# Dense attention scores in one place of two PSUM banks, banded attention with two banks of value sums: another split of the eight banks in a two-layer hybrid encoder on one core

## The chip, the cores and the metric

The kernel runs on one core of a Trainium2 chip. Time is device microseconds of one execution. The kernel before was run three times: 2706.91, 2704.07 and 2705.36 us, so its median is 2705.36 us. One further execution was recorded by the hardware profiler; it took 2709.95 us, and its span, from the first to the last instruction of the program, is 2707.9 us.

## The reference

`x` is 1024 tokens by 1024 features in float32. There are two layers. Each normalises `x`, projects it through one wide matrix, and cuts the result into four groups of four heads:

```
y_a = mla_mixer(...)    # A: latent attention, every query sees all 1024 keys
y_b = diff_mixer(...)   # B: per head two softmaxes over all 1024 keys, w = p0 - lam * p1
y_c = swa_mixer(...)    # C: keys within 128 of the query, with a sink logit
y_d = na_mixer(...)     # D: 8 x 16 neighbourhood on the 64-wide token grid, with a bias table
x = x + concat(norm(y_a), y_b, norm(y_c), norm(y_d)) @ w_out
x = x + square(relu(norm(x) @ w_up)) @ w_down
```

A last normalisation follows. A and B are called dense here, C and D banded. A softmax takes the row's largest score off before the exponential; the kernel finds it as the minimum of the negated scores.

## The kernel before

Each float32 operand of a product is kept as a high and a low part, so that a product is three matmuls per block of 128 rows (`passes`, lines 219 to 224). Half a projected tile is 8 blocks, or 24 matmuls of 512 columns.

In one layer `attention` goes through these stages. Two waves of three tiles make the queries, keys and values of B. Then B runs, then D, then C, then A; beside each of them runs a *fill*: products that the groups after it need. B has the latent projections of A (`proj_latent`) and the projections of D (`proj_d`) as its fill; D has the projections of C (`proj_c`, eight half tiles) and then the second step of A's latents (`latent_up`); C and A have the first half of the output projection (`groups_bd`). `weave` (line 545) puts the calls in turn, a few steps of the main work and then a few of the fill. Behind it a list scheduler sets the final order of each engine's instructions: it takes what is ready by priority (B and D have a lead over their fill), and gives a tile its place in a pool when the place is free. On the chip each engine then runs its list strictly in that order, and waits where an operand or a place is not ready.

PSUM has eight banks of 128 x 512 float32. `banks(mm=2, tr=2, sb=3, pv=1)` at line 426 divides them once for B, D, C and A together: two for products and small matmuls (`mm`), two for transposed probabilities (`tr`), three for scores (`sb`), one for sums of values (`pv`). A tile of one kind waits until an earlier tile at the same place has been read.

Dense attention is done by query tiles of 128 rows. `softmax` (lines 803 to 816) takes the 1024 keys as two halves, each with a bank of its own: matmuls (one per half in B, three in A), then on VectorE (DVE) a scaled copy to `p` that also keeps the running minimum (line 812). The second half starts from the first one's minimum. Then one exponential on ScalarE (ACT) runs over all 1024 (line 815). In B a query tile has two softmaxes; `cb` is the factor for the second one, ACT scales it (line 898) and GpSimd (POOL) adds the two. `dense` then transposes two query tiles together in four steps (`tr`), ACT and DVE make their high and low parts (`pth`, `ptl`), and TensorE (PE) multiplies them by the values (`pv`, lines 834 and 835).

Banded attention (`banded`, lines 966 to 1027) has eight query tiles with at most 384 keys each. Scores of four tiles are made ahead. For key block `kb`, `parts` transposes the probabilities of the up to three query tiles that see it, and `apply` adds their products to a bank of value sums that covers four query tiles. With one such bank the second half can only start when the first is read out: the parts of key blocks 3 and 4 are kept in `held` and applied a second time after that. `zeroed` (line 1032) starts a bank with a matmul of zeros. D's bias tile has six slots of 128 x 128, since a query tile at the edge needs two neighbouring slots of another kind.

Of the kernel before, what the change touches and what calls it, by code (L numbers as in the profile page):

```python
# [21 lines left out]
P = 128  # L22
S = 1024
# [55 lines left out]
def neighbours():  # L79
# [8 lines left out]
    out = np.full((P, 6, P), -1)  # L88
    for slot, ok in enumerate((row_ok & (ck >= c), row_ok, row_ok & (ck < c), row_ok, row_ok, row_ok)):
        at = (rk - r + 7) * 31 + 8 * (slot % 3 - 1) + ck - c + 15  # L90
        out[:, slot] = np.where(np.broadcast_to(ok, (P, P)), at, -1)
# [56 lines left out]
class Trunk:  # L148
# [232 lines left out]
    def attention(self, l):  # L381
# [42 lines left out]
        with ExitStack() as stack, ExitStack() as att:  # L424
            self.ap = att.enter_context(sbuf("att"))
            with self.banks(mm=2, tr=2, sb=3, pv=1):
                with sbuf("proj", "right") as self.pp:
# [10 lines left out]
                    def wave():  # L438
                        return [(self.bank(a), self.bank(b)) for a, b in (("sb", "sb"), ("sb", "tr"), ("tr", "pv"))]
# [24 lines left out]
                    fill = chain(proj_c(), self.latent_up(l, lat, rows, qa, ka, va))  # L464
                    self.weave(self.attn_d(l, qd, kd, vd, y["d"]), fill, self.RD, self.LD, every=self.EV[1])
                gout = lambda n: self.gout[n][:, l]
                self.tails.append(self.mix_group(mix, 2, y["d"], gout("na")))
                wa = stack.enter_context(sbuf("wa", "right"))
                wo = stack.enter_context(sbuf("wo", "right"))
                sums, w_out = [], d["w_out"][l]  # L470

                def groups_bd():

                    for m in range(self.EARLY):
                        x = wo.tile([P, S], F, tag="sum", bufs=self.EARLY, name="sum")
                        self.load(x, saved[m])
                        sums.append(x)
                    while None in mix[:4]:
                        yield True
                    for m, x in enumerate(sums):  # L480
                        ws = self.weights(w_out[m, 0])
                        for n in range(2):
                            ps = self.mm_ps()
                            self.product(ps, ws, mix[:4], n)
                            sl = slice(n * 512, n * 512 + 512)
                            self.tt(x[:, sl], ps, x[:, sl], ALU.add)
                            yield True
# [1011 lines left out]
```

## Time and profile before

| what | value |
|---|---|
| median of three runs | 2705.36 us |
| profiled execution | 2709.95 us, span 2707.9 us |
| PE busy | 2549.6 us, 94% of the span |
| DVE busy | 1943.0 us, 72% |
| ACT busy | 1439.8 us, 53% |
| POOL busy | 1130.9 us, 42% |
| B of the first layer, first to last score matmul | 83.1 to 329.4 us |
| D and C of the first layer, first to last score matmul | 330.0 to 480.0 us |
| A of the first layer, first to last score matmul | 480.1 to 614.5 us |
| the same three in the second layer | 1420.1 to 1668.4, 1669.1 to 1820.0, 1820.3 to 1953.0 us |

A matmul's own time in the profile holds its passage through the array: matmuls of 512 columns are shown with about 0.39 us each but start about 0.23 us apart. So PE can be shown busy while it idles a little between two of them, and the distance of starts is the better price.

### The profile page before, as it was taken

Reading aid. Unit: us, or ns where it says so; the run is one execution under the profiler, and the core shown is the slowest. Engines: PE = TensorE matmul, PEld = TensorE weight load, DVE = VectorE, ACT = ScalarE, POOL = GpSimd, SP = SyncE. Lnnn points to the kernel's source line nnn. Section 1 sums busy time; section 2 is a strip of 40 time slices with the busy share of each in tenths; the row PEclk is TensorE's granted clock in tenths of the full one; section 3 lists DMA queues with packets and bytes.
Section 4 is the critical chain, followed back from the end, with each engine's and each line's share of the span. In section 5 each row is a group of like instructions: output and inputs, shape, how many; then the busy total and the mean of one; then the engine's idle time right before and its main releaser. Section 6 shows DMA issues by size and latency. Waiting matters only on the chain.

```text
span 2707.9 us, 37502 instructions
## 1 busy us (share of the span) xinstructions
PE 2549.6 (94%) x12296; PEld 2112.5 (78%) x12296; DVE 1943.0 (72%) x3379; ACT 1439.8 (53%) x2601; POOL 1130.9 (42%) x754
## 2 busy tenths in 40 slices
PE   8989988999899998999999999889998999999997
PEld 6778876787778887888877788668876788878886
DVE  6777866774966668887567777677749666688775
ACT  4667756664534444444436776566635344444444
POOL 2555642201345554545434656321013455544442
PEclk9989988999999999999998899899999999999998
DMA  5534597222144457444244446962221444664431
GB/s 175 169 107 129 158 287 239 82 89 63 46 144 148 153 170 267 143 142 141 95 139 134 121 113 183 295 202 69 71 71 52 154 153 152 221 221 146 136 105 63
DMA packets 186931, 389.19 MB, mean 144 GB/s; under 512 B 23712, under 2 KB 26736, under 8 KB 186736
## 3 DMA queue, kind: packets, MB, share of 16 engines
q1 hardware_dynamic: 172912, 361.62, 43.2%
q10 hardware_dynamic: 13824, 25.17, 2.7%
q8 instruction: 97, 1.59, 0.2%
q14 instruction: 98, 0.80, 0.1%
HBM read 263.29 MB, written 123.41 MB: 143 GB/s over the span
## 4 chain that ended last, share of the span: by engine, by line
PE 73%; DVE 12%; DMA 6%; ACT 4%; issue 3%; POOL 1%; SPq 0%; DVEq 0%; ACTq 0%; POOLq 0%
PE u L222 8%; PE u L224 8%; PE u L223 8%; PE mm L222 5%; PE mm L223 5%; PE mm L224 5%; PE p L222 5%; PE p L223 5%; PE p L224 5%; PE sb L810 3%; PE tr L846 3%; DVE p L812 2%; DVE part L190 2%; PE pv L835 2%; PE pv L834 2%
## 5 line engine op out<-in xcount | busy, mean ns | idle before, releaser
L190 POOL TENSOR_TENSOR wl<-raw,wh 128x512 fp32r<-128x512 f32 x448 | 632.8, 1413 | 704.8 <-ACT wh L196 691.0
L196 ACT ACTIVATE wh<-raw 128x512 fp32r<-128x512 f32 x448 | 281.5, 629 | 576.2 <-PE u L223 310.9
L190 POOL TENSOR_TENSOR wl<-ws,wh 128x512 fp32r<-128x512 f32 (+1 forms) x112 | 147.3, 1316 | 461.0 <-ACT wh L196 436.1
L222 PE MATMUL u<-far,wh 128*128 128x512 f32 x768 | 301.8, 393 | 11.4 <-ACT ev L1242 8.3
L224 PE MATMUL u<-far,wl 128*128 128x512 f32 x768 | 300.6, 391 | 2.2 <-POOL wl L190 2.2
L190 DVE TENSOR_TENSOR raw<-raw 128x512 f32<-128x512 f32 x256 | 223.1, 877 | 109.1 <-POOL wl L190 55.6
L223 PE MATMUL u<-far,wh 128*128 128x512 f32 x768 | 300.6, 391 | 0.0
L190 DVE TENSOR_TENSOR ptl<-tr,pth 128x512 fp32r<-128x512 f32 (+2 forms) x384 | 238.3, 629 | 68.5 <-ACT pth L196 66.8
L815 ACT ACTIVATE p<-p,nm 128x1024 f32<-128x1024 f32 x192 | 220.2, 1147 | 92.3 <-DVE nm L812 91.6
L196 ACT ACTIVATE pth<-tr 128x512 fp32r<-128x512 f32 (+2 forms) x384 | 205.2, 546 | 108.5 <-PE tr L846 64.9
L222 PE MATMUL p<-far,wh 128*128 128x512 f32 x640 | 252.9, 395 | 7.5 <-DVE ev L190 7.5
L224 PE MATMUL p<-far,wl 128*128 128x512 f32 x640 | 251.5, 393 | 1.5 <-POOL wl L190 1.5
L223 PE MATMUL p<-far,wh 128*128 128x512 f32 x640 | 252.2, 394 | 0.0
L810 PE MATMUL sb<-stack 96*128 96x512 f32 x640 | 217.5, 422 | 22.1 <-DVE nm L812 21.4
L190 DVE TENSOR_TENSOR far<-act,far 128x512 fp32r<-128x512 f32 x224 | 207.3, 955 | 14.7 <-ACT far L196 14.7
L190 POOL TENSOR_TENSOR p<-p 128x1024 f32<-128x1024 f32 x64 | 154.0, 2411 | 129.6 <-ACT p L898 121.3
L222 PEld LDWEIGHTS u<-far,wh 128*128 128x128 f32 x768 | 145.3, 189 | 43.5 <-ACT ev L1242 9.1
L222 PE MATMUL mm<-xh,wh 128*128 128x512 f32 x416 | 170.9, 411 | 0.8 <-DVE part L190 0.3
L224 PEld LDWEIGHTS u<-far,wl 128*128 128x128 f32 x768 | 145.2, 189 | 33.5 <-POOL wl L190 3.0
L812 DVE CUSTOM_DVE_ANT_0 p<-sb,zero,nm 128x512 f32<-128x512 f32 x192 | 142.4, 743 | 37.7 <-PE sb L810 34.6
L223 PEld LDWEIGHTS u<-far,wh 128*128 128x128 f32 x768 | 145.4, 189 | 30.0
L223 PE MATMUL mm<-xl,wh 128*128 128x512 f32 x416 | 167.7, 403 | 0.0
(245 smaller groups left out, 6110.1 us busy)
## 6 DMA issues: line engine op xcount, KB each, us to landing
act<-acts SPq DMA_DIRECT2D x224, 256.0 KB
raw<-in_w_up SPq DMA_DIRECT2D x128, 256.0 KB
acts<-ev SPq DMA_DIRECT2D x128, 256.0 KB
raw<-in_w_down SPq DMA_DIRECT2D x128, 256.0 KB
acts<-ev ACTq DMA_DIRECT2D x96, 256.0 KB
ws<-in_w_in SPq DMA_DIRECT2D x76, 256.0 KB
rz<-drows SPq DMA_DIRECT2D x40, 256.0 KB
stack<-kd SPq DMA_DIRECT2D x32, 256.0 KB
```

Of the source, the lines that this page charges most:

```text
L190: (eng or self.nc.vector).tensor_tensor(out=out, in0=a, in1=b, op=op)
L196: nc.scalar.activation(hi, src, AF.Copy)
L222: mm(ps, w[0], x[0][:, sl], start=start, stop=False)
L223: mm(ps, w[0], x[1][:, sl], start=False, stop=False)
L224: mm(ps, w[1], x[0][:, sl], start=False, stop=stop)
L810: self.nc.tensor.matmul(ps, q[:, qt * P:(qt + 1) * P], k[:, sl], start=i == 0, stop=i == len(passes) - 1)
L812: self.nc.vector.tensor_tensor_reduce(out=p[:, sl], in0=ps, in1=self.zero[:, 0:1].bitcast(F).broadcast_to([P, 512]), scale=-scale, scalar= ...
L815: self.nc.scalar.activation(p, p, AF.Exp, bias=nm[:, 1:2], scale=-1.0, accum_out=z)
L834: nc.tensor.matmul(out, v[:, kt], h[:, sl], start=kt == 0, stop=False)
L835: nc.tensor.matmul(out, v[:, kt], lo[:, sl], start=False, stop=kt == 7)
L846: nc.tensor.transpose(t[:, k * 256 + i * P:k * 256 + (i + 1) * P], p[:, (j * 2 + k) * P:(j * 2 + k + 1) * P], self.ident)
```

## The change

- `softmax` takes one tile of 128 x 1024 that covers two neighbouring banks, writes both halves of the scores into it, and runs one VectorE instruction over 1024 elements with one minimum. `sb` has one such place in the dense stages.
- The banks are divided anew for each stage: `DENSE` (mm 2, tr 3, sb one place of two banks, pv 1) for the waves and B, `BANDED` (mm 2, tr 2, sb 2, pv 2) for D and C, and `DENSE` again for A. Three pools follow each other where there was one.
- `banded` opens the second half's bank at key block 3, while the first is still open, and applies every part once to each half that it belongs to. Nothing is held.
- The bias tile has five slots. An edge tile takes two of them that stand two apart, so `in1` of its VectorE instruction has a step, and the other operands are written as blocks of 128.

```
-            with self.banks(mm=2, tr=2, sb=3, pv=1):
-                with sbuf("proj", "right") as self.pp:
+            with sbuf("proj", "right") as self.pp:
+                with self.banks(**self.DENSE):
...
                     def wave():
-                        return [(self.bank(a), self.bank(b)) for a, b in (("sb", "sb"), ("sb", "tr"), ("tr", "pv"))]
+                        sb = self.bank("sb", (P, S))
+                        return [(sb[:, 0:512], sb[:, 512:S])] + [
+                            (self.bank(a), self.bank(b)) for a, b in (("tr", "tr"), ("tr", "pv"))]
...
-                    fill = chain(proj_c(), self.latent_up(l, lat, rows, qa, ka, va))
-                    self.weave(self.attn_d(l, qd, kd, vd, y["d"]), fill, self.RD, self.LD, every=self.EV[1])
...
+                banded = ExitStack()
+                banded.enter_context(self.banks(**self.BANDED))
+                fill = chain(proj_c(), self.latent_up(l, lat, rows, qa, ka, va))
+                self.weave(self.attn_d(l, qd, kd, vd, y["d"]), fill, self.RD, self.LD, every=self.EV[1])
...
+            self.weave(self.attn_c(l, qc, kc, vc, y["c"]), fill, self.RC, end=False, every=self.EV[2])
+            self.tails.append(self.mix_group(mix, 4, y["c"], gout("swa")))
+            banded.close()
+            with self.banks(**self.DENSE):
                 self.weave(self.attn_a(l, qa, ka, krd, va, y["a"]), fill, self.RA, self.LA, every=self.EV[3])
...
+    DENSE = dict(mm=2, tr=3, sb=1, pv=1)
+    BANDED = dict(mm=2, tr=2, sb=2, pv=2)
...
-        nm, p = self.col("nm", 2), self.ptile()
+        nm, p = self.col("nm"), self.ptile()
+        ps = self.bank("sb", (P, S))
         for n in range(2):
-            ps = self.bank("sb")
             sl = slice(n * 512, n * 512 + 512)
             for i, (q, k) in enumerate(passes):
-                self.nc.tensor.matmul(ps, q[:, qt * P:(qt + 1) * P], k[:, sl],
+                self.nc.tensor.matmul(ps[:, sl], q[:, qt * P:(qt + 1) * P], k[:, sl],
                                       start=i == 0, stop=i == len(passes) - 1)
-            self.nc.vector.tensor_tensor_reduce(
-                out=p[:, sl], in0=ps, in1=self.zero[:, 0:1].bitcast(F).broadcast_to([P, 512]), scale=-scale,
-                scalar=nm[:, 0:1] if n else 3e38, op0=ALU.add, op1=ALU.min, accum_out=nm[:, n:n + 1])
-        self.nc.scalar.activation(p, p, AF.Exp, bias=nm[:, 1:2], scale=-1.0, accum_out=z)
+        self.nc.vector.tensor_tensor_reduce(
+            out=p, in0=ps, in1=self.zero[:, 0:1].bitcast(F).broadcast_to([P, S]), scale=-scale,
+            scalar=3e38, op0=ALU.add, op1=ALU.min, accum_out=nm)
+        self.nc.scalar.activation(p, p, AF.Exp, bias=nm, scale=-1.0, accum_out=z)
...
-        pv = self.zeroed()
-        held = []
+        pv = {}
...
-            if kb in (3, 4):
-                held.append(part)
-            if kb <= 4:
-                apply(pv, 0, kb, part)
-            else:
-                apply(pv, 1, kb, part)
-            if kb == 4:
-                self.pv_out(pv, y, j, 0, grid)
-                pv = self.zeroed()
-                for i, p in enumerate(held):
-                    apply(pv, 1, 3 + i, p)
+            for half in range(2):
+                if half * 3 <= kb <= half * 3 + 4:
+                    if kb == half * 3:
+                        pv[half] = self.zeroed()
+                    apply(pv[half], half, kb, part)
+                    if kb == half * 3 + 4:
+                        self.pv_out(pv[half], y, j, half, grid)
...
-                bias = self.ap.tile([P, 6, P], F, tag="bias", bufs=1, name="bias")
+                bias = self.ap.tile([P, 5, P], F, tag="bias", bufs=1, name="bias")
...
-                    b0 = {0: 4, 7: 3}.get(i, 0)
-                    w = ps.shape[1]
+                    near = bias[:, {0: slice(2, 5, 2), 7: slice(0, 3, 2)}.get(i, slice(1, 4))]
+                    blocks = lambda t: t.rearrange("p (a b) -> p a b", b=P)
...
-                        out=p, in0=ps, in1=bias[:, b0:b0 + w // P].rearrange("p a b -> p (a b)"),
+                        out=blocks(p), in0=blocks(ps), in1=near,
```

The built programs give each place in PSUM. In `DENSE` of the first layer `sb` is banks 0 and 1, `tr` banks 2, 3 and 4, `pv` bank 5 and `mm` banks 6 and 7. In `BANDED` `sb` is banks 0 and 1, `mm` banks 2 and 3, `tr` banks 4 and 5, `pv` banks 6 and 7. So D's first products stand where B's last transposes stood. PE has 12088 matmuls before and after, DVE 384 instructions of line 812 before and 192 after.

The scheduler's order moves with it. The first place is PE where B ends and D begins, in the first layer. Lines 222 to 224 are products (`mm<-xh`, here of `proj_c`), 810 a half of B's scores, 846 transposes, 834 and 835 B's value sums, 982 D's scores. Before:

```order
L834 MATMUL pv<-pth,v 128x256
L835 MATMUL pv<-ptl,v 128x256
L846 MATMUL tr<-ident,p 128x128 x4
L810 MATMUL sb<-stack 128x512
L223 MATMUL mm<-xl_165,wh 128x512
L982 MATMUL sb<-stack 128x256 x2
L224 MATMUL mm<-xh_164,wl 128x512
L222 MATMUL mm<-xh_168,wh 128x512
L223 MATMUL mm<-xl_169,wh 128x512
L224 MATMUL mm<-xh_168,wl 128x512
L982 MATMUL sb<-stack 128x384 x2
```

Of the eight half tiles of `proj_c`, five stand ahead of D's first score and the sixth has begun, among B's last nineteen halves of scores. The same place of the changed kernel (scores at line 992, transposes 856, value sums 844 and 845, products 223 to 225, zeros 1036):

```order
L844 MATMUL pv<-pth,v 128x256
L845 MATMUL pv<-ptl,v 128x256
L844 MATMUL pv<-pth,v 128x256
L845 MATMUL pv<-ptl,v 128x256
L992 MATMUL sb<-stack 128x256 x2
L992 MATMUL sb<-stack 128x384 x2
L1036 MATMUL pv<-zero 128x512
L223 MATMUL mm<-xh_164,wh 128x512
```

This is the first product of `proj_c`: all eight half tiles stand behind B's last value sum. Between the last product of `proj_d` and this row there are 241 matmuls and no product: the scores of B's last 19 tiles (38 of line 820), 93 transposes, 96 value sums, and 14 others (D's first four scores, the zeros and nine small ones). The second layer's order is alike.

The second place is PE inside that stretch, where score tiles (line 820, two matmuls each in B) follow each other:

```order
L844 MATMUL pv<-pth,v 128x256
L845 MATMUL pv<-ptl,v 128x256
L856 MATMUL tr<-ident,p 128x128 x3
L820 MATMUL sb<-stack 128x512 x6
L856 MATMUL tr<-ident,p 128x128 x9
L820 MATMUL sb<-stack 128x512 x2
L844 MATMUL pv<-pth,v 128x256
```

Three tiles, x6, now stand right behind each other and all use banks 0 and 1; before, halves went round three banks.

52 lines of the change are left out of this document (25 added, 27 removed).

## The prediction

> **What bounds the kernel now.** I read the page's busy times first, then a table of the first layer by stage, then in each stage who waits for whom.
>
> ```profile
> span 2707.9 us, 37502 instructions
> ...
> PE 2549.6 (94%) x12296; PEld 2112.5 (78%) x12296; DVE 1943.0 (72%) x3379; ACT 1439.8 (53%) x2601; POOL 1130.9 (42%) x754
> ```
>
> ```profile
> core 0: us, PE busy (x) PEld busy (x) DVE busy (x) ACT busy (x) POOL busy (x), PEclk, DMA share, GB/s
> 150.00:175.00 25.00, 17.39 (x74) 13.62 (x73) 19.61 (x44) 16.45 (x27) 18.99 (x11) 0.73 0.40 105
> 175.00:288.00 113.00, 112.03 (x628) 95.73 (x626) 83.95 (x223) 83.77 (x138) 58.05 (x32) 1.00 0.40 119
> 288.00:330.00 42.00, 42.00 (x223) 35.62 (x224) 32.30 (x80) 28.43 (x45) 29.59 (x19) 1.00 0.52 144
> 330.00:362.00 32.00, 29.75 (x164) 26.01 (x163) 17.82 (x48) 19.07 (x46) 13.74 (x10) 0.95 0.94 254
> 362.00:438.00 76.00, 63.72 (x347) 52.05 (x346) 57.23 (x151) 52.93 (x138) 29.65 (x20) 0.93 0.96 298
> 492.00:631.00 139.00, 131.63 (x826) 112.96 (x825) 104.77 (x231) 90.63 (x160) 12.33 (x8) 1.00 0.23 68
> 675.00:700.00 25.00, 25.00 (x112) 20.64 (x111) 21.55 (x31) 13.52 (x23) 3.88 (x3) 1.00 0.19 65
> ```
>
> While B has products beside it (175 to 330) PE is busy in 154.0 of 155 us and DVE in three quarters: PE sets the pace. Where B lacked products (150 to 175) PE did 74 matmuls in 25 us, at a granted clock of 0.73. D with its latents (362 to 438) leaves PE 12.3 us open. The last row, 112 matmuls of 512 columns in 25 us, prices one at 0.223 us. The feed-forward half is not edited, so only the attention stages, about 83 to 631 us and 1420 to 1969 us, can move.
>
> B's pace, and how much of the products lay under B's end:
>
> ```profile
> 83.00:330.00 247.00, 54.17 (x128) 24.47 (x128) 0.95 0.44 129
> 288.00:330.00 42.00, 7.70 (x19) 3.53 (x19) 1.00 0.52 144
> ```
>
> ```profile
> 288.00:330.00 42.00, 26.10 (x81) 15.03 (x81) 0.00 (x0) 0.00 (x0) 1.00 0.52 144
> ```
>
> The first fence counts halves of B's scores (line 810): 128 in 247 us. A query tile has four, so 32 query tiles took 7.7 us each. The second counts matmuls that read `xh`, two of a product's three: 81 mean 121 matmuls, 27 us of products, in B's last 42 us.
>
> **The change part by part.** Rows for the prices, from the groups by line:
>
> ```profile
> L812 DVE CUSTOM_DVE_ANT_0 p<-sb,zero,nm 128x512 f32<-128x512 f32 x192 | 142.4, 743 | 37.7 <-PE sb L810 34.6
> L812 DVE CUSTOM_DVE_ANT_0 p<-sb,zero 128x512 f32<-128x512 f32 x192 | 129.1, 685 | 35.2 <-PE sb L810 9.7 <-POOL p L190 9.0 <-PE tr L846 8.0
> L812 DVE DVE_READ_ACCUMULATOR2_ANT nm<- 128x1 f32 x384 | 31.3, 82 | 0.0
> L815 ACT ACTIVATE p<-p,nm 128x1024 f32<-128x1024 f32 x192 | 220.2, 1147 | 92.3 <-DVE nm L812 91.6
> L815 ACT ACTIVATION_READ_ACCUMULATOR p<-p,nm 128x1 f32 x192 | 35.9, 187 | 0.0
> L898 ACT ACTIVATE p<-p,cb 128x1024 f32<-128x1024 f32 x64 | 72.9, 1143 | 12.1 <-DVE cb L897 11.1 <-DVE cb L896 0.7
> L196 ACT ACTIVATE pth<-tr 128x512 fp32r<-128x512 f32 (+2 forms) x384 | 205.2, 546 | 108.5 <-PE tr L846 64.9 <-PE tr L991 25.6 <-PE pv L1003 13.1
> L190 POOL TENSOR_TENSOR p<-p 128x1024 f32<-128x1024 f32 x64 | 154.0, 2411 | 129.6 <-ACT p L898 121.3 <-PE mm L222 4.1 <-PE sb L810 3.6
> ```
>
> *One minimum.* A softmax's DVE work is now 685 + 743 + 2 x 82 = 1592 ns. No row shows 1024 elements. Below, one such instruction cannot be shorter than 743 ns; above, it is two of 685 ns. The 384-column banded form (0.548 us median) against 0.685 us for 512 gives 1.07 ns a column, so I take 685 + 512 x 1.07 = 1.23 us, 1.31 with its read. That saves 0.28 us, 53 us of DVE over 192 softmaxes. In B, DVE is not the bound, so this buys nothing there; PE's products cover it.
>
> ```profile
> L1058 DVE CUSTOM_DVE_ANT_0 p<-sb,bias x64: 406/548/558, 333.4 to 1751.0; 128x384 f32<-128x384 f32 x48, 128x256 f32<-128x256 f32 x16
> ```
>
> *One place.* With three banks PE already idles for score places:
>
> ```profile
> PEld sb L810 <- DVE nm L812: 32.4, 36, 5.0
> ...
> PE sb L810 <- DVE nm L812: 21.4, 22, 4.6
> ```
>
> With one place the next tile waits for the whole minimum, about 1.5 us from the last score's start of passage to the release. In the changed order I summed PE's own work between one tile and the next, at the prices here: in a layer's B 26 to 29 of 64 tiles have less than 1.45 us there, some none. Behind a waiting score stand, on PE, transposes and value sums, and for those ACT and DVE. Outside the stretch treated next the shortfalls add up to 12 us; 7 of them lie around the present hole at 150 to 175 us, where PE waits anyway. I take +6 us a layer, bounds 0 and 12.
>
> The Trainium skill (Perfetto Trace Analysis, Optimizing Tensor Performance) says that independent groups of matmuls should go round different banks, so that one's read-out overlaps the next one's matmuls. The trace agrees as far as it goes, since the two waits above exist even with three banks; by the rule alone every one of 192 tiles could pay a whole 1.31 us, an estimate of 250 us where no other work stands between.
>
> *B's end without products.* `proj_c` now starts behind B's last transposes, since D's `mm` banks were B's `tr` banks. So 19 score tiles, 9.5 query tiles, run with no product beside them. What sets their pace then? ACT needs 2 x (1.147 + 0.187) + 1.143 + 2 x 0.546 = 4.9 us a query tile, DVE 2 x 1.31 plus two `ptl` of some 0.63, 3.9 us. The present kernel shows a short burst without products (between the `proj_d` and `proj_c` parts):
>
> ```profile
> 279.76 0.39 PE L810 MATMUL sb<-stack 96*128 96x512 f32 x1
> ...
> 282.84 0.94 PE L810 MATMUL sb<-stack 96*128 96x512 f32 x3
> ...
> 285.42 0.28 PE L834 MATMUL pv<-pth,v 128*128 128x256 f32 x1
> 285.54 0.28 PE L835 MATMUL pv<-ptl,v 128*128 128x256 f32 x1
> 285.66 0.60 PE L846 MATMUL tr<-ident,p 128*128 128x128 f32 x4
> ...
> 286.22 0.40 PE L810 MATMUL sb<-stack 96*128 96x512 f32 x1
> ```
>
> Seven halves start within 6.5 us, under 4 us a query tile, but that is what buffers allow for a moment. I take ACT's 4.9: 9.5 x 4.9 = 47 us, plus the last tile's way out (POOL 2.4, then four steps of transposes and parts at about 1.1), 7 us: 54. Lower bound 9.5 x 4.5 (ACT's reads hidden) + 5 = 48; upper bound today's pace, 9.5 x 7.7 + 7 = 80. Today's end takes 42 us, so +12 (+6 to +38). But it holds 9.5 tiles, not 19: what stands ahead is shorter by 4.75 query tiles. One costs PE 4 x 0.223 for scores, and per step four transposes at (0.60 - 0.27) / 3 = 0.11 and four value sums at 0.12, for two steps: 2.7 us. That is -13.
>
> *Products moved into D.* The 27 us of products now stand among D's heads, whose span today is 330 to 438, with 14.5 us of PE open by the table. Hidden entirely they cost 0, not at all 27. `latent_up` comes after them, and its loads need the places of `proj_c`'s operands, so nothing of it comes earlier; on SP its loads fall behind those of D's later heads, where the DMA share is 0.94 to 0.96. I take 27 - 13 = +14.
>
> *Two value banks, two score banks, five slots.* The bank of zeros is waited for like this:
>
> ```profile
> L1032 PE MATMUL pv<-zero x32: 376/483/774, 363.1 to 1844.5; 128*128 128x512 f32 x32
> ...
>   DVE y L190: 13.5, 17
>   DVE yc L190: 3.4, 9
> ```
>
> At most 17 us in the kernel, 8 a layer; a stall removed there lets the next transposes arrive, for which ACT and DVE are then late, so I take -4. The third score bank's loss is 0 to 3, taken as 2. The bias load is shorter by a sixth, and waits for it end in 7.4 us at most over both layers: nothing. The stepped operand on DVE could cost or save a few tens of ns in 16 edge tiles: nothing.
>
> *A.* 32 tiles a layer; 7 to 12 have too little work between, by 5 us (0 to 11). DVE gets 32 x 0.28 = 9 us lighter, and `tr` has a third bank, against waits for DVE and ACT in a stage where PE is shown idle 7.4 us of 139: -4 (-9 to 0). Sum of this and the part before: -1, from -17 to +14.
>
> **Sum.** A layer: +6 + 12 - 13 + 14 - 1 = +18 us; both: +36. The profiled execution, 2709.95, would become 2746; it lies 4.6 over the median of the runs, 2705.4, which would become 2741.
>
> **The rivals.**
>
> *B's end at today's pace.* If latency through `p`'s six places (score, minimum, exponential, factor, POOL's sum of 2.4 us, transposes) sets B and not ACT, the end takes 80 us: 26 more a layer, 2793. For it: the hole at 150 to 175 was as slow. Against it: there POOL was busy 19 of 25 us with other work, and the burst at 280 was fast.
>
> *D takes the products for nothing* (the other side). D's heads wait on DMA, DVE and each other and not on PE, so its open time swallows all 27 us, and then the value banks give their full 8 a layer, without a loss from the scores' third bank; of the score waits only 2 us remain, those around the present hole being swallowed too. The sum is 2 + 12 - 13 + 0 - 8 + 1 = -6 a layer, 2693. It decides from the point where less than about 3 us of the 27 stay visible. For it: the DMA share near 1, and D's pace of 27 us a head (108 by 4). Against it: the table shows 14.5 us of PE open, half of what it needs.
>
> *DVE was the bound.* Then its 53 us come out of the span: 2652. For it: the exponential waits 91.6 us for the minimum in the row of line 815. Against it: 154 of 155 us of PE.
>
> The Trainium skill (Perfetto Trace Analysis, Optimizing Scalar/DVE Operations) says that larger operations raise throughput where the engine is saturated, and that where it is not, but causes bubbles elsewhere, breaking instructions up may let work finish sooner. DVE's 72% puts this kernel on the second side, which speaks against the change.
>
> *The pieces cancel*: B's end takes 48 and the products cost 2, so 6 + 6 - 13 + 2 - 1 = 0: 2705. Nothing speaks for it but the size of the bounds.
>
> **How the numbers follow.** Forecast 0.49; B's end at today's pace 0.15; D takes all 0.16; DVE bound 0.06; cancelling 0.14. About 0.2%, 5.4 us, is what a measurement here can tell from no change. So slower 0.64, same 0.14, faster 0.22. All lower bounds together give 0 + 6 - 13 + 0 - 17 = -24 a layer, 2657; all upper bounds 12 + 38 - 13 + 27 + 14 = +78, 2861. The range of 8 in 10 is 2690 to 2795: it leaves out DVE as the bound, nearly half of the case with D, and what lies beyond a slow end. The forecast's own range is 2718 to 2765, half of each bound taken.
>
> **What would show it.** Right, if products (`mm<-xh`) are absent for some 50 us before D's first score, the score halves there keep 4.5 to 6 us a query tile, and waits of `sb` for `nm` grow from 54 to over 90 us. Line 812's successor should show about 1.23 us for 1024 elements. D's span should grow by 10 to 20 us with PE fuller; the waits of `pv<-zero` should vanish. It is wrong if PE stays full to B's last score, if the stretch takes under 45 us, or if A shortens by more than 8 us.

## The result, and the profile after

The changed kernel takes 2848.02 us (median of four runs, 2842.53 to 2853.89). The kernel before, run beside it, takes 2706.14 us. The ratio is 1.0521, with a 95% interval from 1.0495 to 1.0548: the change makes the kernel 5.2% slower. The forecast was 2741, the range 2690 to 2795. The direction was right, and the loss is four times as large: +142 us instead of +36. No rival that was written down gives it either.

The page of the changed kernel, its first two rows on the span and the engines:

```profile
span 2846.0 us, 37064 instructions
...
PE 2603.1 (91%) x12296; PEld 2141.2 (75%) x12296; DVE 1925.3 (68%) x2995; ACT 1440.1 (51%) x2601; POOL 1132.3 (40%) x754
```

The groups by line (busy us, mean ns of one, then idle time before them and what ended it):

```profile
L822 DVE CUSTOM_DVE_ANT_0 p<-sb,zero 128x1024 f32<-128x1024 f32 x192 | 234.2, 1220 | 129.5 <-PE sb L820 128.2 <-issue 0.3
L825 ACT ACTIVATE p<-p,nm 128x1024 f32<-128x1024 f32 x192 | 220.2, 1147 | 117.0 <-DVE nm L822 116.6
L820 PE MATMUL sb<-stack 96*128 96x512 f32 x640 | 208.7, 437 | 49.4 <-DVE nm L822 48.7
...
L820 PEld LDWEIGHTS sb<-stack 96*128 96x128 f32 x640 | 115.9, 202 | 84.8 <-DVE nm L822 69.5
```

The minimum over 1024 elements takes 1220 ns, as the estimate of 1.23 had it, and VectorE's scores cost 234.2 us where two halves cost 142.4 + 129.1. No gain from that saving is to be seen: the minimum now waits 128.2 us for scores, and scores wait 48.7 + 69.5 = 118 us for minima, where it was 54 (the rows of PE and of its weight loads added as in the prediction; in time they overlap, so such sums compare kernels and are not a loss in us).

The stages of the first layer, as one table of windows:

```profile
core 0: us, PE busy (x) PEld busy (x) DVE busy (x) ACT busy (x) POOL busy (x), PEclk, DMA share, GB/s
...
150.00:250.00 100.00, 87.28 (x428) 70.26 (x427) 65.23 (x135) 68.62 (x111) 52.26 (x29) 0.88 0.37 106
250.00:295.00 45.00, 45.00 (x238) 38.44 (x237) 26.11 (x50) 26.52 (x45) 23.25 (x13) 1.00 0.30 101
295.00:365.00 70.00, 47.83 (x241) 36.84 (x240) 45.35 (x92) 49.30 (x79) 27.17 (x12) 0.80 0.40 106
365.00:424.00 59.00, 58.16 (x293) 49.01 (x292) 29.84 (x71) 25.98 (x64) 25.91 (x20) 1.00 0.63 176
424.00:496.00 72.00, 53.58 (x283) 44.37 (x282) 48.23 (x123) 42.93 (x112) 23.65 (x17) 0.88 0.93 281
496.00:522.00 26.00, 21.60 (x123) 15.98 (x121) 20.41 (x64) 21.28 (x59) 7.71 (x6) 1.00 0.94 285
522.00:557.00 35.00, 26.14 (x121) 20.68 (x121) 20.42 (x38) 15.68 (x33) 10.48 (x5) 0.80 0.29 81
557.00:690.00 133.00, 124.36 (x745) 108.86 (x746) 90.23 (x148) 78.74 (x140) 12.34 (x8) 0.95 0.25 71
```

There are two holes. The first is B's end: 241 matmuls in 70 us (295 to 365), with none of `proj_c` among them, as the same window for the tile `xh` shows (its one matmul is the last before the stretch):

```profile
295.20:365.60 70.40, 0.24 (x1) 0.19 (x1) 0.00 (x0) 0.00 (x0) 0.81 0.40 105
```

B's last 38 halves of scores lie in the 55 us from 295 to 350 (the window for line 820); the other 15 us are the way out, in which hardly anything but transposes and value sums of the last tiles is left:

```profile
295.00:350.00 55.00, 16.29 (x38) 6.88 (x37) 0.81 0.35 98
```

The second hole is 522 to 557: 121 matmuls in 35 us, between C's last score (522.2) and A's first (557.2). Before, A's first score came at 480.1, right behind C's last at 480.0. The hole holds the transposes and value sums of C's last tiles, 24 matmuls of the output projection and a few small ones. For the operands of that projection (`mixh`, `mixl`) TensorE also waits in it:

```profile
541.73 1.11 PE L223 MATMUL mm<-mixh,wh 128*128 128x512 f32 x2 [3.19 <-ACT mixh L200]
543.84 0.79 PE L224 MATMUL mm<-mixl,wh 128*128 128x512 f32 x1 [1.00 <-DVE mixl L201]
...
546.61 0.79 PE L224 MATMUL mm<-mixl,wh 128*128 128x512 f32 x1 [1.55 <-DVE mixl L201]
```

The layer can be cut at four starts that every kernel has. From B's first score to D's first it takes 281.6 us against 246.9 (+35), from there to C's last score 157.6 against 150.0 (+8), from there to A's first score 35.0 against 0.2 (+35), and from there to the first matmul of the feed-forward 212.1 against 219.0 (-7). That is +70 in the first layer. In the second it is 687 us against 619, +68, with nearly the same four parts (+32, +10, +34, -8).

### The profile page after: what moved, and what is told of

It is laid out like the page before. It is cut to its first block, busy times and chain, and to the rows that moved or that the text cites. A ratio compares the mean times of both kernels' runs of the same rounds, so it can differ in the third digit from the quotient of the medians.

```text
span 2846.0 us, 37064 instructions
## 1 busy us (share of the span) xinstructions
PE 2603.1 (91%) x12296; PEld 2141.2 (75%) x12296; DVE 1925.3 (68%) x2995; ACT 1440.1 (51%) x2601; POOL 1132.3 (40%) x754
## 5 line engine op out<-in xcount | busy, mean ns | idle before, releaser
L822 DVE CUSTOM_DVE_ANT_0 p<-sb,zero 128x1024 f32<-128x1024 f32 x192 | 234.2, 1220 | 129.5 <-PE sb L820 128.2
L820 PE MATMUL sb<-stack 96*128 96x512 f32 x640 | 208.7, 437 | 49.4 <-DVE nm L822 48.7
L856 PE MATMUL tr<-ident,p 128*128 128x128 f32 x1024 | 169.7, 294 | 33.0 <-POOL p L191 17.4
L820 PEld LDWEIGHTS sb<-stack 96*128 96x128 f32 x640 | 115.9, 202 | 84.8 <-DVE nm L822 69.5
L223 PEld LDWEIGHTS u<-far,wh 128*128 128x128 f32 x768 | 145.2, 189 | 42.4 <-ACT ev L1246 9.1
L856 PEld LDWEIGHTS tr<-ident,p 128*128 128x128 f32 x1024 | 132.3, 152 | 54.2 <-POOL p L191 22.2
```

The source lines that it names most:

```text
L223: mm(ps, w[0], x[0][:, sl], start=start, stop=False)
L820: self.nc.tensor.matmul(ps[:, sl], q[:, qt * P:(qt + 1) * P], k[:, sl], start=i == 0, stop=i == len(passes) - 1)
L822: self.nc.vector.tensor_tensor_reduce(out=p, in0=ps, in1=self.zero[:, 0:1].bitcast(F).broadcast_to([P, S]), scale=-scale, scalar=3e38, op0 ...
L856: nc.tensor.transpose(t[:, k * 256 + i * P:k * 256 + (i + 1) * P], p[:, (j * 2 + k) * P:(j * 2 + k + 1) * P], self.ident)
```

## The experiments

Two causes are in question. **Seams**: three PSUM pools follow each other instead of one, so that nothing of a later pool would start before the earlier one's last work. **Places**: dense scores have one place of two banks instead of three banks that go round. The rivals to them are parts that were changed along: the length of the minimum, the value banks, the bias slots. In the table, B is its first to last score, D and C the first score of D to the last of C, A its first to last score, all of the first layer in us; "layer" runs from B's first score to the first matmul of the feed-forward, in both layers. Ratios are to the kernel before, run beside it.

| kernel | ratio, 95% interval | B | D, C | A | layer |
|---|---|---|---|---|---|
| before | 1 | 246 | 150 | 134 | 616 / 619 |
| changed | 1.0521, 1.0495 to 1.0548 | 267 | 158 | 133 | 686 / 687 |
| e1, both seams alone | 1.0307, 1.0286 to 1.0328 | 232 | 172 | 126 | 654 / 658 |
| f2, seam before D alone | 1.0218, 1.0189 to 1.0247 | 230 | 179 | 134 | 645 / 648 |
| e5, seam before A alone | 1.0124, 1.0092 to 1.0156 | 245 | 149 | 125 | 627 / 632 |
| e2, one place and one minimum, one pool | 1.0311, 1.0286 to 1.0335 | 291 | 215 | 134 | 661 / 658 |
| e6, one place and two minima, one pool | 1.0777, 1.0736 to 1.0818 | 341 | 204 | 157 | 721 / 720 |
| f1, two places and one minimum, one pool | 1.0396, 1.0371 to 1.0422 | 225 | 200 | 149 | 668 / 672 |
| f3, changed, but two single banks and two minima | 1.0330, 1.0314 to 1.0347 | 261 | 158 | 124 | 670 / 665 |
| e3, changed, with product banks in a pool of their own | 1.0319, 1.0293 to 1.0345 | 296 | 116 | 130 | 660 / 663 |
| e4, two score and two value banks, one pool | 1.0121, 1.0100 to 1.0141 | 272 | 133 | 129 | 629 / 635 |
| e7, five bias slots alone | 1.0035, 1.0019 to 1.0051 | 244 | 150 | 139 | 618 / 621 |
| e8, second value bank from the score banks, one pool | 0.9965, 0.9947 to 0.9983 | 246 | 139 | 134 | 608 / 613 |

B and D can't be compared alone where the products stand elsewhere: in e1 and f2 B is short because products have left it, in e3 three quarters of `proj_c` run in B and the rest before D, and in e2 and e6 D's first scores lie inside B. So here are the four parts of the layer for the kernels in which they follow each other (first / second layer, us). The last column counts the matmuls of `proj_c` that start after D's first score, in the first layer; there are 192 in all.

| kernel | B's first score to D's first | to C's last score | to A's first score | to the feed-forward | products after D's start |
|---|---|---|---|---|---|
| before | 247 / 249 | 150 / 151 | 0 / 0 | 219 / 219 | 70 |
| changed | 282 / 281 | 158 / 161 | 35 / 34 | 212 / 211 | 192 |
| e1, both seams | 250 / 248 | 172 / 176 | 22 / 24 | 211 / 210 | 192 |
| f2, seam before D | 248 / 247 | 179 / 179 | 0 / 0 | 218 / 222 | 192 |
| e5, seam before A | 245 / 247 | 149 / 154 | 22 / 19 | 210 / 211 | 70 |
| f3 | 277 / 273 | 158 / 165 | 32 / 22 | 203 / 204 | 192 |
| e3 | 320 / 320 | 116 / 119 | 16 / 17 | 208 / 208 | 0 |
| e4 | 281 / 282 | 133 / 136 | 3 / 3 | 212 / 214 | 27 |
| e8 | 246 / 243 | 139 / 132 | 3 / 9 | 219 / 229 | 70 |

### e1: both seams, and nothing else

```
-            with self.banks(mm=2, tr=2, sb=3, pv=1):
...
+                with self.banks(**self.DENSE):
...
+                banded.enter_context(self.banks(**self.BANDED))
...
+            banded.close()
+            with self.banks(**self.DENSE):
...
+    DENSE = dict(mm=2, tr=2, sb=3, pv=1)
+    BANDED = dict(mm=2, tr=2, sb=3, pv=1)
```

> The kernel before with nothing changed but that its one pool of banks is closed and opened again, with the same split (mm 2, tr 2, sb 3, pv 1), between B and D and between C and A. Theory S (the loss comes from the two seams, at which nothing of the next stage may stand among the last work of the stage before): in the order 25 us of PE work at B's end have no product, and A's first score stands behind C's last value sum, as in the changed kernel; 80 to 120 us of the 142 lost, so about 2790 to 2825 us. Rival P (the loss comes from the single place for scores): within 15 us of before, 2706 to 2720.

The ratio is 1.0307: some 83 us from closing and opening a pool of the very same split. The windows of e1 from B's last score on, to D's first score, the end of the products, C's last score, and A's first:

```profile
315.00:334.00 19.00, 13.93 (x63) 11.26 (x62) 8.44 (x20) 10.08 (x17) 4.67 (x2) 0.73 0.50 111
334.00:393.00 59.00, 58.30 (x294) 49.16 (x293) 29.75 (x71) 25.15 (x63) 25.46 (x19) 1.00 0.63 179
...
505.00:527.00 22.00, 16.09 (x87) 12.53 (x87) 13.76 (x30) 11.89 (x28) 4.19 (x2) 0.92 0.30 78
```

The same two holes are there with the old split of the banks, and the rival that put the loss on the score places alone (2706 to 2720) is refuted. In the kernel before, A's first score stands 141 matmuls (29 us) ahead of C's last value sum; in e1 and in the changed kernel it stands behind it.

The prediction put the products' delay down to places: D's `mm` banks lie where B's `tr` banks lay. e1 doesn't exclude that for the products, since in its built program, too, D's `mm` banks are 3 and 4, which were B's `tr`. But places aren't the whole of it, as D's scores show. They use banks 0 to 2, B's own score banks, and B's last score starts at 315.0. Still D's first score comes only behind B's last value sum, which uses bank 5:

```profile
333.42 0.28 PE L842 MATMUL pv<-ptl,v 128*128 128x256 f32 x1
333.54 1.10 PE L989 MATMUL sb<-stack 128*128 128x256 f32 x6
```

In e1 and f2, in both layers, this distance is 0.12 us. In e5, with no seam here, D's first score stands 25 us ahead of B's last value sum. So a closed pool is a wall for the next pool's work even in banks that have long been free.

### f2 and e5: one seam at a time

```
 f2: banded = ExitStack(); banded.enter_context(self.banks(...))   # opened before D, kept for A
 e5: banded.close()                                                # one pool for B, D, C; a new one for A
     with self.banks(...): self.weave(self.attn_a(...))
```

> The kernel before with the pool closed and opened again between B and D alone. If the two seams add up (theory), this costs what both together cost less what the one before A costs: 2788.8 - 2738.6 = 50, so 2755, with products missing in B's last 26 us of PE's work and 20 to 35 us later as the last product ends. If the stall at the one seam is partly what the other one shows (rival), it is above 2770.

> The kernel before with one pool for the waves, B, D and C, closed and opened again with the same split only between C and A. In the run with both seams A's first score came 22 us after C's last in each layer, where before it came at once, and A was then 8 us shorter. If the seams' costs add up, this one costs 10 to 15 us a layer, 2725 to 2735 us, and the seam at B's end the other 50 to 60 us. If work of C's end only moves, nothing: 2700 to 2711.

The seam before D costs 2.18%, 59 us, the one before A 1.24%, 34 us. Together that is 3.42% against e1's 3.07%, so they add up within their intervals. (f2's 2766 us lies between the two expectations, 2755 and 2770; e5's 2739 is a little over its 2725 to 2735, and its traced execution, 5 us faster than the median, shows 11 and 13 us a layer.) The wait that the prediction left out entirely, A's start, is over a third of the two. In f2 the windows of B's end and of D with C read:

```profile
316.00:334.00 18.00, 13.41 (x55) 10.45 (x55) 8.15 (x20) 9.53 (x16) 4.66 (x2) 0.62 0.51 115
...
333.50:513.50 180.00, 148.34 (x740) 121.83 (x740) 104.71 (x266) 94.89 (x242) 63.56 (x43) 0.90 0.77 220
```

The same window of the kernel before:

```profile
330.00:480.00 150.00, 127.76 (x669) 106.42 (x667) 99.25 (x264) 96.01 (x245) 52.80 (x33) 0.90 0.85 255
```

By the counts, 122 products moved into D; D and C have only 71 matmuls more because some 50 of B's last transposes and value sums, which ran behind D's first score before, now stand ahead of it. The products are 27 us at 0.223 us each, and D with C is 28 to 29 us longer. So D hides none of them. Nor does B's side gain by losing them: its scores are done 16 us earlier in the first layer (230 us), but its way out, 16 to 19 us that ran beside D before, now stands alone ahead of D's first score. From B's first score to D's first it takes 248 and 247 us, where it took 247 and 249.

### e3: the seams taken off the products

```
+        if tag == "mm" and self.mmp is not None:
+            return self.mmp.tile(list(shape), F, tag=tag, bufs=2, name=tag)
...
+            self.mmp = mm_pool.enter_context(self.tc.tile_pool(
...
+            mm_pool.close()
+            self.mmp = None
...
+    DENSE = dict(tr=3, sb=1, pv=1)
+    BANDED = dict(tr=2, sb=2, pv=2)
```

> The changed kernel, but the two banks for products are a pool of their own that lasts through all of attention; the other three kinds still change pools at both seams. In the order the products of C stand among B's last scores again, A's first score still stands behind C's last value sum. Theory S: the part of the loss at B's end comes back, 40 to 80 us, so 2770 to 2810; what is left is the seam before A and the single place. Rival P: as the changed kernel, 2835 to 2860.

With only the product banks outside the seams, products run on under B's end (they end at 400 us, three before D's first score at 403), and 5.21% becomes 3.19%: 55 us come back. By the parts of the layer it is chance that this is about what the seam before D costs alone. Against the changed kernel, the first layer is 38 us longer up to D's first score and 42 us shorter from there to C's last, which is the price of 192 products moved from one side to the other; 18 us come back in the hole before A, and 4 behind it. There, too, the pool of their own lets products move: 12 of the output projection stand in the hole instead of 24. So with the one place products cost about as much ahead of D as in it, and most of what comes back comes back at the seam before A.

### e2, e6, f1: how scores are placed, without a seam

```
 e2: self.banks(mm=2, tr=2, sb=1, xb=1, pv=1)    # sb: one place of two banks; one minimum
 e6: as e2, with the two minima of 512 back
 f1: self.banks(mm=1, tr=2, sb=2, pv=1)          # two places of two banks, paid by one product bank
```

> One pool for all of attention, and only the scores changed: one place of two banks with one minimum for B and A, and one further bank, so that C and D put their scores in turn into that bank and into the first half of the place; value sums as before. Theory S: no seam, so 10 to 50 us slower than before from waits for the place, 2716 to 2756. Rival P: most of the loss, 2800 to 2850. If DVE's 0.28 us per softmax counted, it would be faster than 2700.

> As the run with one place and no seam, but each half of the place has its own minimum as in the kernel before, so DVE does the old work and the place is still free only after the second half. Theory W (what costs is the number of places: the next tile's scores cannot be made while this one is read): as slow as with one minimum, 2780 to 2810. Rival M (what costs is the long instruction, behind which other DVE work waits): back to 2710 to 2750.

> One pool for all of attention, one minimum over 1024, but two places of two banks each (paid for with one of the two banks for products). If B's loss comes from having one score tile under way at a time (theory: places), B is back at 245 to 260 us, less what the missing product bank costs, and the whole lies between 2690 and 2740. If the loss comes from the long minimum itself (rival: a bank is given back only after 1.22 us instead of 0.7), B stays near the 291 us of one place and the whole is above 2770.

`xb` is one bank more, for every second score tile of C and D; the other tiles use the place. So in e2 and e6 C and D have lost a score place as well. The waits of scores for minima in e2, e6 and f1, in this order:

```profile
PEld sb L812 <- DVE nm L814: 62.1, 86, 4.6
PE sb L812 <- DVE nm L814: 35.8, 49, 3.9
```

```profile
PEld sb L813 <- DVE nm L815: 141.6, 160, 2.4
PE sb L813 <- DVE nm L815: 90.0, 110, 2.2
```

```profile
PEld sb L811 <- DVE nm L813: 43.4, 56, 7.7
...
PE sb L811 <- DVE nm L813: 25.0, 29, 7.3
```

One place without any seam costs 3.11%, 84 us, with 98 us of such waits instead of 54, and B takes 291 us for nearly the work it did in 246. At 2791 us e2 lies outside both expectations: the price is well over the 10 to 50 us of the theory that blamed the seams, and under that of its rival, since each cause has its share. With two minima in the same place the waits are 232 us and the loss 7.77%, more than either expectation had. The rows of e6 in order of time show why that is not only a matter of VectorE's 0.3 us a tile:

```profile
206.72 0.68 DVE L815 CUSTOM_DVE_ANT_0 p<-sb,zero 128x512 f32<-128x512 f32 x1
...
207.47 0.50 PE L813 MATMUL sb<-stack 96*128 96x512 f32 x1 [1.03 <-DVE nm L815]
208.01 0.75 DVE L815 CUSTOM_DVE_ANT_0 p<-sb,zero,nm 128x512 f32<-128x512 f32 x1 [0.60 <-PE sb L813]
...
208.82 0.49 PE L813 MATMUL sb<-stack 96*128 96x512 f32 x1 [0.85 <-DVE nm L815]
209.35 0.69 DVE L815 CUSTOM_DVE_ANT_0 p<-sb,zero 128x512 f32<-128x512 f32 x1 [0.59 <-PE sb L813]
```

Every half waits for the minimum of the half before it, also within one tile: the place is one tile, and its second bank is not written while its first is read. So e6 isn't a clean price of the long minimum. It shows that, given one place, one minimum is much the better way to use it.

f1 gives a second place, and the waits fall from 98 to 68 us. That speaks for the number of tiles under way, though f1 is slower elsewhere, which leaves scores more time. The total is 1.0396, far over the 2690 to 2740 that the theory gave, most likely because the bank taken from the products costs more than the place brings. In f1 products wait for their single bank to be read:

```profile
PE mm L222 <- DVE both L190: 15.6, 3, 9.8
...
PE mm L222 <- ACT mixh L199: 11.9, 3, 5.9
...
PE mm L222 <- DVE part L190: 11.7, 12, 2.3
```

In the kernel before, the second of these took 4.4 us and the third 1.2. D with C is 50 us longer, with 785 matmuls in it instead of 669, since all of `proj_c` stands behind D's first score here, without any seam. A is 15 us longer, with 22 products of the output projection more. f1's question (whether the long minimum alone would harm) stays half open: the waits answer it, the time does not.

### f3: the changed kernel with its two score banks as single places

```
-    DENSE = dict(mm=2, tr=3, sb=1, pv=1)      # sb: one place of two banks, one minimum
+    DENSE = dict(mm=2, tr=3, sb=2, pv=1)      # sb: two places of one bank, two minima
```

> The changed kernel, with its two banks of dense scores used as two single places and two minima again; seams, value banks, third transpose bank and bias slots stay. Theory (places and seams are two separate losses): B is 20 to 25 us shorter in each layer than in the changed kernel, and the whole is 2795 to 2810. Rival (with the seams there, the score places no longer matter, since B's end is slow for another reason): within 10 us of the changed kernel's 2848.

The same two banks, used as two places with two minima, bring 5.21% down to 3.30%: the one place with its one minimum is worth 1.9%, 52 us, beside the seams too. The time is as expected (2795), but its place is not: B, which was to be 20 to 25 us shorter a layer, is 5 and 9. Another 6 to 7 us a layer lie ahead of B's first score, 7 to 9 behind A's first score, and the rest in the hole before A. Its waits:

```profile
PEld sb L818 <- DVE nm L820: 42.2, 69, 2.0
PE sb L818 <- DVE nm L820: 19.1, 41, 1.5
```

That is 61 us against 118. What is left over e1 (3.30 less 3.07%) is the net of the third score bank's loss, the second value bank, the third transpose bank and the bias slots: 6 us in the whole kernel, which the intervals don't tell from nothing.

### e4 and e8: the value banks, without a seam

```
 e4: self.banks(mm=2, tr=2, sb=2, pv=2)                      # nothing held
 e8: self.banks(mm=2, tr=2, sb=3, pv=1)                      # as before, nothing held
     pv[half] = self.zeroed("sb" if half else "pv")          # second half's sums in a score bank
```

> One pool for all of attention with mm 2, tr 2, sb 2 (single banks, two minima as before), pv 2; the banded part opens its second bank of value sums early and holds nothing. Theory S: no seam; the waits for the bank of zeros (17 us) go, two score banks in place of three cost a little in B: 2690 to 2725. Rival P says nothing of it, as there is no single place.

> The kernel before, one pool and the old split, with nothing held: the second half's bank of value sums is opened at key block 3 in one of the three score banks. B keeps its three score banks. In the run with two value banks and no seam D and C took 133 to 136 us in place of 150 while B lost 26. Theory W: D and C gain 12 to 17 us a layer and B loses nothing: 2670 to 2685. Rival: a score bank given to sums costs D and C what the second sum gains: 2700 to 2720.

In e4 D and C take 133 us instead of 150, and B 272 instead of 246. Part of both is moved work: 43 products (10 us) have left D, and 23 of them (5 us) stand in B. So two value banks gain some 7 us a layer, the third score bank is worth some 21, and the kernel is 1.2% slower, where 2690 to 2725 us was expected. e8 keeps three banks for the scores of B and A, and borrows one of them where D and C need a second bank of sums. It is the one kernel that beats both, if by little: 2696.70 us over ten runs, ratio 0.9965, at most 0.9983; 2670 to 2685 was expected. D and C, in the first layer:

```profile
330.50:470.50 140.00, 123.72 (x669) 103.60 (x668) 98.66 (x264) 94.50 (x244) 48.25 (x31) 0.91 0.92 268
```

The same 669 matmuls take 140 us, where they took 150; the second layer has 132 us against 151, with 42 matmuls fewer. The zeros' waits for `y` and `yc`, 13.5 and 3.4 us before, are down to 4.2 and 0.5. The profiles show 14 us for the two layers (8 and 6), the medians 10; what D and C gain in the second layer A gives back in part (143 us from its first to its last score, 133 before).

### e7: five bias slots alone

```
-                bias = self.ap.tile([P, 6, P], F, tag="bias", bufs=1, name="bias")
+                bias = self.ap.tile([P, 5, P], F, tag="bias", bufs=1, name="bias")
```

> The kernel before with the five bias slots and the stepped operand alone. All theories: no change, 2700 to 2711; the stepped VectorE instruction of line 1058 or its successor within 20 ns of 548.

The prediction had nothing for it, and it costs 0.35% (10 us, ten runs). In the profiles the difference is spread: 3 us before B's first score, 2 in each layer's attention. The stepped operand is no reason by its own price: the 16 instructions of 256 columns take 421 ns in the mean in e7 and before. VectorE waits 17.9 us for the bias load, where it waited 7.4; but in e5, with six slots, it waits 17.2. The order of C's end moved by eight matmuls. Which of this makes the 10 us isn't settled.

## Why the prediction missed

The prediction's +18 us a layer and the measured +70 (first layer) can be laid over the four parts of the layer. Up to D's first score it had 6 + 12 - 13 = 5 and it is 35. From there to C's last score it had 14 - 4 + 2 = 12 and it is 8. For the hole before A it had nothing and it is 35. For A it had 5 - 4 = 1 and it is -7, the hole's work that is no longer there.

By causes, from e1 over f3 to the changed kernel, it is 41.5 us a layer for the seams (half of 83), 3 for the banks and slots and 26 for the one place. That these add up to 70.5 follows from how they are formed; that the traces of the two kernels have 70 and 68 agrees.

**The seam before D: 13 predicted, 29 measured (f2).** What the order showed was read rightly, products leave B's end and go into D. B's side was right in sum: 12 - 13 = -1 predicted, +1 and -2 measured in f2. What was mis-sized is *products in D*, put at 27 - 13 = 14, their price less nearly all that PE had open there. f2 shows that the open time can't be used so, since D with C grew by 28 to 29 us. A reason that fits, though no run isolates it, is that PE's gaps in D are waits inside short chains, where a product delays the next link. The bound "not at all 27" was the right value.

That D and C then come out at 8 to 10 us, near the 12 of the prediction, is luck: the products cost twice their term, and in the changed kernel something gives that back. The two value banks do a part of it (by this reading 7 us a layer in e4, and 5 a layer in e8's median, where 4 was put down). Besides, 22 products of the output projection (5 us) that ran under C before now stand in the hole. The rest wasn't separated.

The two terms of B's side were right only together. *B's end* was put at 54 us, and takes 70.4 in the changed kernel. Scores went at (350 - 295) / 9.5 = 5.8 us a query tile, not at ACT's 4.9, and the way out took 15 us, not 7. The one place is not the main reason: in e1 and f2, with three banks, the 24 halves of such a stretch take 30 to 32 us, 5.1 to 5.4 us a query tile. ACT was busy 49 of 70 us and bound nothing; neither did another engine, the row 295 to 365 has none over 50. What is left is the chain of one tile through all engines, as the rival with 7.7 us had it; that was argued from this row and not tried apart. A burst of 6.5 us was taken as evidence for a stretch of 55; besides, products run until 282.0 in it, so that only five of its seven halves had none beside them.

**The seam before A: nothing predicted, 17 measured (half of e5's 1.24%).** The prediction asked only what D's new pool does. The same pool change stands between C and A. Alone it opens a hole of 19 to 22 us, of which A gives back 7 to 9. In the changed kernel the hole is 35 us, from 522 to 557, since products of the output projection that wait for their operands stand in it as well. It was to be seen in the order, by the same reading that found B's end: before, A's first score stands ahead of C's last value sum.

**The one place: 7 predicted, 26 measured against two single places (after against f3), 42 against three (half of e2's 84 us, where C and D lose a place, too).** This is the largest error, and most of the 30 us by which the part up to D's first score was put too low: a seam leaves that part as it was (e1, f2), and fewer score places make it longer (277 in f3, 282 in the changed kernel, against 247). The step "the next tile waits for the whole minimum, about 1.5 us from the last score's start of passage to the release" is wrong in its size. In the changed kernel's B, in the first layer, the time from there to the end of the minimum with its read is 1.89 us at the median and 2.26 in the mean of 64 tiles. A short piece of it, in order of time:

```profile
215.47 0.99 PE L820 MATMUL sb<-stack 96*128 96x512 f32 x2
...
217.46 1.22 DVE L822 CUSTOM_DVE_ANT_0 p<-sb,zero 128x1024 f32<-128x1024 f32 x1
...
218.74 0.74 PE L820 MATMUL sb<-stack 96*128 96x512 f32 x2 [0.65 <-DVE nm L822]
...
219.91 1.21 DVE L822 CUSTOM_DVE_ANT_0 p<-sb,zero 128x1024 f32<-128x1024 f32 x1
...
221.19 0.74 PE L820 MATMUL sb<-stack 96*128 96x512 f32 x2 [0.40 <-DVE nm L822]
...
221.96 1.23 DVE L822 CUSTOM_DVE_ANT_0 p<-sb,zero 128x1024 f32<-128x1024 f32 x1 [0.83 <-PE sb L820]
...
223.25 0.73 PE L820 MATMUL sb<-stack 96*128 96x512 f32 x2 [0.34 <-DVE nm L822]
```

With VectorE free, the minimum starts 0.43 us behind the last score's start at the earliest, and the place is handed on 2.06 us after it was taken (221.19 to 223.25). But in 34 of the 64 tiles the minimum starts over 0.6 us behind, and in 27 of these VectorE is still at other work when the scores have passed; the tile of 215.47 holds its place for 3.27 us. A buffer is held for the reader's queue too, not for the reader's instruction alone, and the prediction priced the instruction. The Trainium skill (Perfetto Trace Analysis, Optimizing Tensor Performance) says that independent groups of matmuls should go round different banks. By that rule the change looked bad, and f3 agrees: 61 us of waits with two places and 118 with one.

**Banks and slots: -2 predicted, +3 measured (f3 against e1), but these are not the same sum.** f3 has also lost the third score bank of B and A, worth some 21 us in e4's B, which the prediction had in its term for the one place. It has two value banks, put at -4 by the waits of their zeros, and a third transpose bank, and both give that back: from A's first score to the feed-forward f3 takes 8 and 6 us less than e1, and ahead of B's first score 6 to 7. The 2 us for the third score bank in D and C were not tried apart. What was to vanish did not: in the changed kernel the zeros wait 12.9 us for `y`,

```profile
  DVE y L191: 12.9, 4
```

now in four long waits instead of 17 short ones.

**The rivals.** *B's end at today's pace* was nearest, but the end is only 16 us over the 54 of the prediction, and 52 us a layer were missing. *D takes the products for nothing* is refuted by f2. *DVE was the bound* is refuted by e2: the 53 us were saved there as well, and the kernel is 84 us slower. Whether the larger operation itself does harm, as the prediction's second rule would have it, stays open: after against f3 changes it together with the places, and given one place, one long minimum (e2) is much faster than two (e6). Apart from all this, the forecast's own range, 2718 to 2765, is not half of each bound; half of them all is 2699 to 2801, still far below 2848.

Of the signs set down, these came as said: no product before D's first score in 70 us, the score halves' 5.8 us a query tile, waits of `sb` for `nm` over 90, the minimum of 1.22 us. D, from its first score to C's first, took 93 us instead of 76, within the 10 to 20 more that were named, though C gave half of it back. The waits of the zeros did not vanish. The 70 us and the 118 us of waits were asked for from below only, so those signs could not tell a small loss from a large one.

## What to carry to other kernels

A pool that is closed and opened again was a wall for this scheduler, even with the same split of banks: look at the order on both sides of every such wall. Price each one by how long the last work of the old pool then runs alone (16 to 19 us of B's way out in f2), and don't count on the next stage to hide the work that was moved (D hid nothing of 27 us). A buffer's price is the time it is held, with the reader's queue in it, times how many are under way; taking a bank from one use to give to another wants a price for the giver of the same care as for the receiver. Idle time of an engine in a stage is not by itself room for moved work. And compare kernels by parts between the same starts: a total that fits (e3's 55 us, D and C's 8) can come from elsewhere.

## What was not expected of the hardware

In the holes the granted clock falls, too, as TensorE's load does. Windows of ten to fifteen microseconds at the start of B's end in the changed kernel:

```profile
285.00:300.00 15.00, 13.92 (x84) 11.71 (x82) 11.87 (x21) 9.29 (x18) 5.01 (x4) 1.00 0.34 109
300.00:310.00 10.00, 6.79 (x27) 4.13 (x26) 7.61 (x18) 7.75 (x12) 4.51 (x2) 0.74 1.04 286
310.00:320.00 10.00, 5.82 (x26) 5.12 (x26) 6.16 (x14) 7.74 (x12) 3.11 (x3) 0.67 0.31 73
320.00:330.00 10.00, 6.29 (x29) 5.00 (x29) 4.49 (x10) 4.51 (x9) 4.04 (x2) 0.73 0.32 107
```

With the clock, the same instruction gets longer: C's transposes right before and within the second hole (minimum, median, maximum in ns) are

```profile
L1001 PE MATMUL tr<-ident,p x10: 270/272/300, 516.2 to 519.9; 128*128 128x128 f32 x10
```

```profile
L1001 PE MATMUL tr<-ident,p x16: 270/372/421, 530.1 to 536.9; 128*128 128x128 f32 x16
```

So a hole can cost a little more than its idle time: work in it is slower. The Trainium skill (TensorE: Matmul & The Clock Gate, Part 1: The HAM clock gate) says that a hardware monitor sets the clock by how busy the array has been recently, and these rows agree with it. How much of the 142 us this makes was not tried apart.
